# RMS norm with repeated rows: a first load in three transfers, gamma in two, one VectorE copy in two

## The chip, the cores and the metric

The kernel runs on one core of a Trainium2 chip. The core has a tensor engine (unused here), VectorE (DVE in the profile), ScalarE (ACT), GpSimd (POOL) and SyncE (SP), and 16 DMA engines that carry all traffic between HBM and the on-chip memory (SBUF, 128 partitions). DMAs are issued from an engine's own instruction queue: here SP issues the loads of x and all stores, and ACT issues the loads of gamma. The metric is the device time of one execution in microseconds (us); the number for a kernel is the median of several runs. A profile is one further execution, recorded.

## The reference

```python
def reference(x, gamma):              # x: 8 x 512 x 2048 f32, gamma: 2048 f32
    x_rep = np.repeat(x, 2, axis=1)
    rms = np.sqrt((x_rep ** 2).mean(axis=-1, keepdims=True) + 1e-6)
    x_norm = x_rep / rms
    return (x_norm * gamma[None, None, :]).astype(np.float32)
```

Each row of 2048 numbers is divided by its root mean square, multiplied by gamma, and written twice, in two neighbouring rows of the output. So 33.5 MB are read and 67.1 MB are written.

## The kernel before

**Tiling.** The 4096 rows of x are cut into four tiles of 1024. A tile puts 8 consecutive rows (`H * K`, H = 2, K = 4) on each of the 128 partitions: 64 KB of contiguous HBM per partition, 8 MB in all. A row of x becomes two output rows, so a tile makes two stores of 8 MB, one for each half `h` of its 8 rows.

**Buffers.** One SBUF array `y` holds three areas of 8 rows a partition: `first` at 0, `second` at 8, `third` at 16. The even tile of a pair is loaded at `first + K`, so its rows 0 to 3 lie in the upper half of `first` and its rows 4 to 7 in the lower half of `second`. The odd tile fills `third`. The scaled rows are written back into the same array: result row k goes to place 2k of the area that is stored, and its copy to place 2k + 1.

**Helpers.** `load` (L49 to L52) issues a tile's load on SP. Its argument `cuts` names the row numbers at which the load is cut into transfers, and the transfers are issued in reversed order, the last rows first. `squares` (L58 to L70) runs on ACT: for each row a Square with a running sum (L65, its output is thrown away in `sq`), then one Sqrt over the sums (L69). `scale` (L72 to L82) runs on VectorE: a reciprocal (L78) and, for each row, one instruction that multiplies by it and by gamma (L79). `repeat` (L84 to L86) copies finished rows to their neighbouring places, on the engine whose copy it is given, so that L86 appears for both ACT and VectorE. `store` (L54 to L57) issues a store on SP.

**Order.** The schedule is written by hand (`manual_schedule`), so instructions run on each engine in the order of the program. `four(n, constants, cuts, at_once)` handles the pair of tiles n and n + 1, and is called twice, for tiles 0 and 1 and for tiles 2 and 3. It loads the even tile, runs `constants`, loads the odd tile, and then works through four halves, each of which ends with a store: rows 0 to 3 of the even tile (in two groups of two rows), rows 4 to 7 of it in descending order, and the two halves of the odd tile. In the first two halves the copies are shared by ACT and VectorE: In the first of them ACT copies rows 0 and 1 and VectorE rows 2 and 3; in the second ACT copies rows 2 and 3 and VectorE rows 0 and 1. ACT takes `at_once` rows in an instruction, VectorE two.

**SP's queue.** SP holds, in this order, the first pair's loads, four stores, the second pair's two loads and four stores. A store waits until its copies are done. The load of tile 2 goes where the third store reads, and waits for it; the load of tile 3 likewise waits for the fourth store.

**The first call** gets `cuts` of (7, 8): row 7 of every partition goes first as a transfer of 1 MB, then rows 0 to 6 as one of 7 MB; its `at_once` is 1. The second call, for tiles 2 and 3, loads a tile in one transfer and has an `at_once` of 2 (`half`).

**Gamma** comes in through one partition and is spread to all 128 by GpSimd. `G` is 16 and `E` is 2, so `C = D // G - E` is 126. One DMA (L128) brings the first 16 x 126 = 2016 numbers, as 16 chunks of 126 in places 256 numbers apart; `E` further DMAs (L134) bring 16 numbers each. GpSimd spreads the 2016 with one broadcast (L138) and the last 32 with another (L142). The staging places lie in `y` rows 0 to 2 of partition 0, which are overwritten later by the first results. After that ACT does a Sqrt on one number (L145), for which its table is loaded.

Of the kernel before, what the change touches and what calls it, by code (L numbers as in the profile page):

```python
# [1 line left out]

# [4 lines left out]


@with_exitstack
def kernel(  # L10
    ctx: ExitStack,
    tc: tile.TileContext,
    x: bass.AP,
    gamma: bass.AP,
    out: bass.AP,
):
    nc = tc.nc
    P = nc.NUM_PARTITIONS
    f32 = mybir.dt.float32
    Act = mybir.ActivationFunctionType  # L20
    Alu = mybir.AluOpType

    B, S, D = x.shape
    Bo, So, Do = out.shape
    R = So // S
    assert R == 2 and D == Do and B == Bo and So == S * R
    eps = 1e-6
    inv_d = 1.0 / float(D)


    K = 4
    N = B * S
    ntiles = N // (P * K)
    assert N % (P * K) == 0 and ntiles == 8
    H = 2
    x_t = x.rearrange("b s d -> (b s) d").rearrange("(n p k) d -> n p k d", p=P, k=H * K)
    out_t = out.rearrange("b s d -> (b s) d").rearrange("(n p h j) d -> n h p (j d)", p=P, h=H, j=K * R)

    singles = ctx.enter_context(tc.tile_pool(name="singles", bufs=1))
    rows = ctx.enter_context(tc.tile_pool(name="rows", bufs=1))  # L40
    junk = ctx.enter_context(tc.tile_pool(name="junk", bufs=1, space=bass.MemoryType.PSUM))
    small = ctx.enter_context(tc.tile_pool(name="small", bufs=4))

    y = rows.tile([P, 3 * K * R, D], f32, name="y")
    first, second, third = 0, K * R, 2 * K * R

    def load(n, at, cuts=(H * K,)):  # L49
        ends = (0, *cuts)  # L50
        for k0, k1 in reversed(list(zip(ends, ends[1:]))):
            nc.sync.dma_start(out=y[:, at + k0 : at + k1, :], in_=x_t[n][:, k0:k1, :])  # L52

    def store(n, h, to):  # L54
        nc.sync.dma_start(
            out=out_t[n, h], in_=y[:, to : to + K * R, :].rearrange("p j d -> p (j d)")
        )  # L57

    def squares(at, rows):

        n = len(rows)
        ss = small.tile([P, n], f32, name=f"ss{n}")
        for c, k in enumerate(rows):
            sq = junk.tile([P, D], f32, name="sq")
            nc.scalar.activation(  # L65
                out=sq[:], in_=y[:, at + k, :], func=Act.Square, accum_out=ss[:, c : c + 1]
            )
        rms = small.tile([P, n], f32, name=f"rms{n}")
        nc.scalar.activation(out=rms[:], in_=ss[:], func=Act.Sqrt, scale=inv_d, bias=eps_t[:])  # L69
        return rms  # L70

    def scale(at, to, rows, rms, at_once=K):  # L72
        n = len(rows)
        rstd = small.tile([P, n], f32, name=f"rstd{n}")
        for c, k in enumerate(rows):
            if c % at_once == 0:
                part = slice(c, min(c + at_once, n))
                nc.vector.reciprocal(out=rstd[:, part], in_=rms[:, part])  # L78
            nc.vector.scalar_tensor_tensor(  # L79
                out=y[:, to + R * k, :], in0=y[:, at + k, :], scalar=rstd[:, c : c + 1],  # L80
                in1=gamma_b[:], op0=Alu.mult, op1=Alu.mult,
            )  # L82

    def repeat(to, k0, k1, copy):  # L84
        y_r = y[:, to + R * k0 : to + R * k1, :].rearrange("p (k r) d -> p k r d", r=R)
        copy(out=y_r[:, :, 1, :], in_=y_r[:, :, 0, :])  # L86

    ctx.enter_context(tc.manual_schedule())

    half = K // 2  # L90
    up, down = list(range(K)), list(range(K - 1, -1, -1))

    def four(n, constants, cuts, at_once):


        load(n, first + K, cuts)
        constants()
        load(n + 1, third)
        for rows, n_at_once in ((up[:half], half), (up[half:], at_once)):
            scale(first + K, first, rows, squares(first + K, rows), n_at_once)  # L100
        for k in range(0, half, at_once):
            repeat(first, k, k + at_once, nc.scalar.copy)
        repeat(first, half, K, nc.vector.tensor_copy)
        store(n, 0, first)
        scale(second, second, down, squares(second, down))
        for k in range(half, K, at_once):
            repeat(second, k, k + at_once, nc.scalar.copy)
        repeat(second, 0, half, nc.vector.tensor_copy)
        store(n, 1, second)
        roots = [squares(third + h * K, up) for h in range(H)]  # L110
        scale(third, first, up, roots[0])
        repeat(first, 0, half, nc.scalar.copy)
        repeat(first, half, K, nc.scalar.copy)
        store(n + 1, 0, first)
        scale(third + K, third, up, roots[1])
        repeat(third, 0, K, nc.scalar.copy)
        store(n + 1, 1, third)

    gamma_b = singles.tile([P, D], f32, name="gamma_b")
    G, E = 16, 2  # L120
    C = D // G - E
    gamma_s = y[0:1, 0:2, :].rearrange("p k (c d) -> p (k c) d", c=G // 2)
    gamma_t = y[0:1, 2, :]
    eps_t = singles.tile([P, 1], f32, name="eps_t")

    def constants():
        nc.gpsimd.memset(eps_t, eps)  # L127
        nc.scalar.dma_start(  # L128
            out=gamma_s[0:1, :, :C],
            in_=gamma[: G * C].rearrange("(p c d) -> p c d", p=1, c=G),  # L130
        )
        for c in range(E):
            at = G * C + c * G
            nc.scalar.dma_start(  # L134
                out=gamma_t[0:1, c * G : (c + 1) * G],
                in_=gamma[at : at + G].partition_broadcast(1),
            )
        nc.gpsimd.partition_broadcast(  # L138
            out_ap=gamma_b[:, : G * C].rearrange("p (c d) -> p c d", c=G),
            in_ap=gamma_s[0:1, :, :C],  # L140
        )
        nc.gpsimd.partition_broadcast(out_ap=gamma_b[:, G * C :], in_ap=gamma_t[0:1, : E * G])  # L142

        root = singles.tile([P, 1], f32, name="root")[:]
        nc.scalar.activation(out=root, in_=eps_t[:], func=Act.Sqrt)  # L145

    four(0, constants, (H * K - 1, H * K), 1)
    four(2, lambda: None, (H * K,), half)


# [1 line left out]
_INS = ['x', 'gamma']  # L152
_OUTS = [((8, 1024, 2048), 'float32')]


# [23 lines left out]
```

## Time and profile before

| what | value |
|---|---|
| median of 3 runs | 238.25 us (238.18 to 238.48) |
| profiled execution: its own time | 239.85 us |
| profiled execution: span, first to last instruction | 238.0 us |
| ACT copies of 128x4096 (6) / 128x2048 (4), mean of one | 3.598 us / 1.892 us |
| VectorE copies of 128x4096 (4), mean of one | 2.293 us |
| VectorE multiply (L79), mean of one of 32 | 2.349 us |
| load of row 7, issue to landing | 4.9 us |
| load of rows 0 to 6, issue to landing | 21.5 us |

A group of the profile is named by line, engine and operation, and what it writes and reads, with partitions x elements. An engine with a q behind its name (SPq, ACTq) is the sequencer that issues, here DMAs. A wait is shown as the idle time before an instruction and, after an arrow, what ended it. The share of the DMA engines is the mean over all 16 of them; since a window counts a packet where it begins, and a large packet takes over two microseconds, short windows go over 1.00 and under it.

### The profile page before, as it was taken

The page shows a single profiled execution, that of the slowest core. Times are in us where ns is not written, and L with a number is a line of the kernel's source. Part 1 is how long each engine was busy: PE and PEld are TensorE (multiplying, and loading weights), DVE is VectorE, ACT ScalarE, POOL GpSimd, SP SyncE. Part 2 cuts the span into 40 slices and gives each one's busy share as a digit, 9 for nine tenths or more (in the row PEclk, how much of TensorE's full clock was granted, in tenths as well). Part 3 has the DMA queues.
Part 4 walks back from the last instruction along what each step waited for, and adds up shares of the span by engine and source line. Part 5 has one row for each costly group of instructions (what it writes and reads, how often), then busy time and mean ns, then how long its engine had stood idle before and what let it go on. Part 6 is the DMA issues. An engine that isn't in the chain of part 4 may idle for free.

```text
span 238.0 us, 228 instructions
## 1 busy us (share of the span) xinstructions
DVE 84.4 (35%) x47; ACT 110.2 (46%) x88; POOL 2.9 (1%) x7
## 2 busy tenths in 40 slices
DVE  0000495792799400000000006937918992000000
ACT  2001999299996560000000039891999957400000
POOL 0300000000000000000000000000000000000000
DMA  8997989898998989898999999999998999999994
GB/s 332 463 453 340 529 352 529 352 518 363 463 419 365 518 352 529 352 529 352 419 386 430 441 441 441 430 452 408 463 419 386 474 408 463 419 441 441 441 441 176
DMA packets 1909, 100.68 MB, mean 423 GB/s; under 512 B 244, under 2 KB 244, under 8 KB 244
## 3 DMA queue, kind: packets, MB, share of 16 engines
q1 hardware_dynamic: 1872, 100.66, 98.4%
q10 hardware_dynamic: 36, 0.01, 0.0%
q14 instruction: 1, 0.01, 0.0%
HBM read 33.56 MB, written 67.11 MB: 423 GB/s over the span
## 4 chain that ended last, share of the span: by engine, by line
DMA 46%; ACT 28%; DVE 11%; issue 1%; SPq 0%; DVEq 0%; ACTq 0%
DMA y<-in_x_dram 26%; DMA out_dram<-y 20%; ACT sq L65 17%; DVE y L79 11%; ACT y L86 11%; ACT rms L69 1%; DVE rstd L78 0%; SPq L52 0%; DVEq L79 0%; ACTq L86 0%
## 5 line engine op out<-in xcount | busy, mean ns | idle before, releaser
L65 ACT ACTIVATE sq<-y 128x2048 f32<-128x2048 f32 x32 | 60.1, 1878 | 73.2 <-DMA y<-in_x_dram 72.5
L79 DVE SCALAR_TENSOR_TENSOR y<-y,rstd,gamma_b 128x2048 f32<-128x2048 f32 x32 | 73.8, 2349 | 2.2 <-DMA out_dram<-y 1.6
L86 ACT COPY y<-y 128x4096 f32<-128x4096 f32 (+2 forms) x12 | 42.8, 3599 | 18.9 <-DVE y L79 18.9
L78 DVE RECIPROCAL rstd<-rms 128x4 f32<-128x4 f32 (+2 forms) x11 | 1.9, 169 | 111.2 <-ACT rms L69 111.2
L86 DVE COPY y<-y 128x4096 f32<-128x4096 f32 x4 | 9.2, 2293 | 0.1
L65 ACT ACTIVATION_READ_ACCUMULATOR sq<-y 128x1 f32 x32 | 6.0, 186 | 0.0
L69 ACT ACTIVATE rms<-ss,eps_t 128x4 f32<-128x4 f32 (+1 forms) x10 | 3.0, 297 | 0.3
L145 ACT ACT_TABLE_LOAD x1 | 1.3, 1283 | 2.3 <-issue 2.3
L138 POOL PARTITION_BROADCAST gamma_b<-y x1 | 2.3, 2257 | 5.1 <-DMA y<-in_gamma_dram 5.1
L142 POOL PARTITION_BROADCAST gamma_b<-y x1 | 0.3, 310 | 6.2 <-DMA y<-in_gamma_dram 6.2
L145 ACT ACTIVATE root<-eps_t 128x1 f32<-128x1 f32 x1 | 0.2, 203 | 0.0
L127 POOL MEMSET eps_t<- 128x1 f32 x1 | 0.1, 98 | 0.3 <-POOLq L163 0.3
L163 POOL MEMSET const-bfloat16-1.0<- 128x1 bf16 x1 | 0.1, 101 | 0.0
L163 POOL MEMSET const-uint8-127<- 128x1 uint8 x1 | 0.1, 101 | 0.0
L163 POOL MEMSET const-float32-0.0<- 128x1 f32 x1 | 0.1, 98 | 0.2 <-issue 0.2
L163 POOL MEMSET const-float32-1.0<- 128x1 f32 x1 | 0.1, 98 | 0.0
## 6 DMA issues: line engine op xcount, KB each, us to landing
y<-in_x_dram SPq DMA_DIRECT2D x1, 7168.0 KB, 21.5
y<-in_x_dram SPq DMA_DIRECT2D x1, 1024.0 KB, 4.9
out_dram<-y SPq DMA_DIRECT2D x8, 24.9
y<-in_x_dram SPq DMA_DIRECT2D x3, 40.5
y<-in_gamma_dram ACTq DMA_DIRECT2D x2, 0.1 KB
y<-in_gamma_dram ACTq DMA_DIRECT2D x1, 7.9 KB, 5.1
```

Source lines behind the costliest of these rows:

```text
L65: nc.scalar.activation(out=sq[:], in_=y[:, at + k, :], func=Act.Square, accum_out=ss[:, c : c + 1])
L69: nc.scalar.activation(out=rms[:], in_=ss[:], func=Act.Sqrt, scale=inv_d, bias=eps_t[:])
L78: nc.vector.reciprocal(out=rstd[:, part], in_=rms[:, part])
L79: nc.vector.scalar_tensor_tensor(out=y[:, to + R * k, :], in0=y[:, at + k, :], scalar=rstd[:, c : c + 1], in1=gamma_b[:], op0=Alu.mult, op ...
L86: copy(out=y_r[:, :, 1, :], in_=y_r[:, :, 0, :])
L127: nc.gpsimd.memset(eps_t, eps)
L138: nc.gpsimd.partition_broadcast(out_ap=gamma_b[:, : G * C].rearrange("p (c d) -> p c d", c=G), in_ap=gamma_s[0:1, :, :C],)
L142: nc.gpsimd.partition_broadcast(out_ap=gamma_b[:, G * C :], in_ap=gamma_t[0:1, : E * G])
L145: nc.scalar.activation(out=root, in_=eps_t[:], func=Act.Sqrt)
L163: nc = _bacc.Bacc("TRN2", target_bir_lowering=False, num_devices=1)
```

## The change

Three things change.

1. The first call's `cuts` are (6, 7, 8): row 7, row 6 and rows 0 to 5 are loaded as three transfers in that order, of 1, 1 and 6 MB.
2. `E` is 1, so `C` is 127: the first gamma DMA brings 16 chunks of 127 numbers, one DMA brings the last 16, and GpSimd's broadcasts spread 2032 and 16 numbers.
3. VectorE's copy in the second half of the even tile is made in steps of `K - 1 - at_once` rows. That is 2 in the first call, where the copy stays one instruction, and 1 in the second call, where it becomes two instructions of one row each.

The number of DMAs in the program stays 16: one more load, one gamma transfer less.

```diff
@@ four()
         scale(second, second, down, squares(second, down))
         for k in range(half, K, at_once):
             repeat(second, k, k + at_once, nc.scalar.copy)
-        repeat(second, 0, half, nc.vector.tensor_copy)
+        step = K - 1 - at_once
+        for k in range(0, half, step):
+            repeat(second, k, k + step, nc.vector.tensor_copy)
         store(n, 1, second)
@@ gamma
-    G, E = 16, 2
+    G, E = 16, 1
     C = D // G - E
@@ calls
-    four(0, constants, (H * K - 1, H * K), 1)
+    four(0, constants, (H * K - 2, H * K - 1, H * K), 1)
     four(2, lambda: None, (H * K,), half)
```

## The prediction

> **What bounds the kernel now.** I read the page's utilisation first, then its DMA part, the timeline of instructions, and the windows view of the DMA engines last.
>
> ```profile
> DVE 84.4 (35%) x47; ACT 110.2 (46%) x88; POOL 2.9 (1%) x7
> ...
> q1 hardware_dynamic: 1872, 100.66, 98.4%
> q10 hardware_dynamic: 36, 0.01, 0.0%
> ...
> HBM read 33.56 MB, written 67.11 MB: 423 GB/s over the span
> ```
>
> No compute engine is busy half of the span, and the packets of the SP queue (q1) take 98.4% of all 16 DMA engines' time. The floor is 100.66 MB through those engines. An edit can act in two ways: it changes the work that the engines carry, or it makes a transfer reach the queue after the queue ran dry. The timeline answers the second:
>
> ```profile
> 0.72 1.34 SPq L52 DMA_DIRECT2D y<-in_x_dram  x3
> 0.72 0.60 ACTq L128 DMA_DIRECT2D y<-in_gamma_dram  x1
> 1.35 0.91 ACTq L134 DMA_DIRECT2D y<-in_gamma_dram  x2
> 2.29 1.28 ACT L145 ACT_TABLE_LOAD   x1 [2.29 <-issue]
> ...
> 14.36 0.31 POOL L142 PARTITION_BROADCAST gamma_b<-y  x1 [6.18 <-DMA y<-in_gamma_dram]
> 22.69 1.88 ACT L65 ACTIVATE sq<-y 128x2048 f32<-128x2048 f32 x1 [18.90 <-DMA y<-in_x_dram]
> ```
>
> The reader sees start, length, engine and line. All three early loads (row 7, rows 0 to 6, the whole second tile) are issued by 2.06 us; ACT's first square waits until 22.69 for rows 0 to 6. The last windows show where the DMA engines lose time (columns: stretch, length, DVE, ACT and POOL busy with counts, clock, DMA share, GB/s):
>
> ```profile
> 101.00:116.00 15.00, 0.00 (x0) 0.00 (x0) 0.00 (x0) 1.00 0.98 424
> 116.00:124.00 8.00, 0.00 (x0) 0.00 (x0) 0.00 (x0) 1.00 1.05 393
> 124.00:138.00 14.00, 0.00 (x0) 0.00 (x0) 0.00 (x0) 1.00 1.03 445
> ```
>
> At 116 to 124 the engines are full but move only 393 GB/s. There the fourth store ends and the load of tile 2 begins. The packet records say the same: a 65,536-byte packet takes 2.418 us nearly everywhere, and 2.6 to 3.9 us in this stretch. The engines, 0.4 us apart before it, leave it 1.7 us apart and end between 235.4 and 236.8 us. The last engine's last store lands at 237.17, which ends the span of 238.0.
>
> **Row 6 as a transfer of its own.** Issue: one more DMA instruction on SP, 0.37 to 0.44 us like the three there. Row 6 takes the slot at 1.14; rows 0 to 5 move to about 1.6, the second tile's load to about 2.1. Behind them SP only waits for the first store, issued at 39.29. The engines reach rows 0 to 5 when rows 7 and 6 are done, near 7.1 us (row 7's packets end at 4.6 to 5.1, and row 6 adds eight of 0.309 us): 5 us of cover, so nothing. Without cover it would be 0.42 us.
>
> Work: each engine carries 8 more packets. From the records an 8,192-byte packet takes 0.309 us and one of 57,344 bytes 2.113 us start to start. The difference, 1.804 us, is 49,152 bytes, exactly rows 0 to 5; what 8,192 bytes then take is 0.301, so 0.008 us is fixed. Rows 6 and 0 to 5 cost 0.309 + 1.812 = 2.121 against 2.113: 0.008 x 8 = 0.066 us an engine, plus one 4-byte completion packet of 0.009: **+0.075 us**. The engines never idle after it, so all of this reaches the end. Bounds: 0 from below (same bytes, same engines; a gain by shifted phases is a rival); from above +0.8 us, if row 6 starts as cold as row 7 did, whose first packets took up to 1.116 instead of 0.309. I take 0.075, since in the record rows 0 to 6 follow row 7's completion packet without a gap.
>
> A rule speaks against the split. The Trainium skill, "DMA: Bandwidth & Descriptors", section "Bandwidth", asks for at least 1 MiB a transfer and measures 6.15 us for 1 MB alone; "Anatomy of one DMA" puts about 2.0 us of fixed cost on each. Row 7 was just such a 1 MiB transfer, 4.9 us from issue to landing, but its packets were busy for 2.5 us and the next transfer's followed them at once. By the rule paid in full the sum would be about 2 us more; the trace lets the fixed part lie beside the next transfer.
>
> **Gamma.** ACT issues two DMAs instead of three: 0.21 to 0.67 us less of the stretch 0.72 to 2.26. Behind them stand the table load and a small root, then ACT is idle for 18.90 us: nothing gained. On the DMA engines, 16 packets grow from 504 to 508 bytes (0.027 us each, no change seen), and one engine loses a 64-byte packet (0.011) and its completion (0.009). Beside the small packets that engine's large ones took 2.235, 2.126, 2.125 and 2.121 us, not 2.116: 0.14 us in all. One of two such DMAs goes: half of that 0.14 and of 0.04 for its four small packets, **-0.09 us on this one engine**, bounds 0 and -0.18. It is the engine that lands last in the first load (22.67; the others by 22.39). At the end it is ahead of the next by only 0.07 us, so the end gains at most that; I take -0.02. POOL's two broadcasts are done by 14.67 and first needed at 27.35, so neither 127-wide chunks nor a shorter second broadcast reach the path; with the cover gone the second would cost its 0.31 us.
>
> **VectorE's copy.** The step K - 1 - at_once is 2 in the first call of four, which keeps one copy, and 1 in the second call: there the copy at 171.32 becomes two of 128x2048. No VectorE row has that form. Below: twice half of 2.293 us, +0. Above: two at the price of the multiply of that form, 2.349 each, +2.41. ACT's copies give 2 x 1.892 - 3.598 = +0.19, and VectorE's smallest instruction, the reciprocal, takes 0.16; I take +0.16. The sixth store's issue moves from 173.69 to 173.85. Store five's issue at 157.04 reached an engine 0.88 us later, so store six is there by 174.7; the earliest engine finishes store five at 177.3. Cover 2.6 us, enough even for +2.41. VectorE's next instruction waits anyway (5.03 us idle until 178.64). **Nothing.** With cover gone it is 0.16 us.
>
> **Sum.** The profiled execution has a span of 238.00 us and a time of its own of 239.85; the runs have a median of 238.25. +0.075 - 0.02 + 0 = +0.05 us: span 238.05, median **238.3**. The first squares move with the load, to about 22.7. Store one then arrives at 40.2 (39.29 + 0.88) where the earliest engine ends the second tile's load at 40.95; both move together, so its 0.8 us of cover stays.
>
> **Rivals.** 0.2% of 238.25 is 0.48 us, about what a measurement of this kernel can tell from no change.
>
> 1. The turn from stores to loads at 116 to 124 comes out better. The edits change by tenths of a microsecond how far the 16 engines stand apart, and that turn decides which engine ends last. For: it is the only lossy place, and the engines leave it 1.4 us apart at the end. Against: the runs shown, 238.18 to 238.48, stay within 0.30 although the start, with first packets of 0.41 to 1.12 us, looks irregular. If the loss were even, the last engine would end near the middle of 235.4 and 236.8 us, 0.7 less: 237.6, or 237.4 with what the gamma engine gains.
>
> 2. The same turn comes out worse. The quickest engines lose about 0.6 us there, the slowest 2.0 (from 99.56 to 140.22 instead of two times 19.32). If the slowest loses another 0.6 to 0.7, 238.9. It decides once the last engine loses 0.45 us more than now. For and against as above.
>
> 3. The slow side by a mechanism: a third transfer ahead of the first square starts in the open. Place: between row 7 and row 6, or row 6 and rows 0 to 5. Price: 0.8 us each if the engines start cold as at 1.7 us, 2.4 if each pays what row 7 paid beyond its packets (4.9 - 2.5), so 239.1 to 240.7. It decides once descriptors come later than 4.6 us for row 6, that is 2.6 us later than its issue plus 0.88 says. Against: no gap at the one seam that there is. The skill's fixed cost, above, would be paid here.
>
> 4. The split copy delays the sixth store: it decides from +2.6 us on 2.293, beyond the upper bound. The time would then be 238.3 plus what exceeds it. I give it no more than the rounding.
>
> That the edit does not do what it says can be only so far: the first call's copy stays whole.
>
> **How the numbers follow.** Forecast 0.64; rival 1 0.16; rival 2 0.13; rivals 3 and 4 together 0.07. Faster by over 0.2% is rival 1, 0.16; slower is rivals 2 to 4, 0.20; same 0.64. The likeliest alone gives 238.1 to 238.6 (the split 0 to 0.3, the spread of runs). The range goes down to 237.6, the middle case of rival 1, and up to 238.9, rival 2's price, leaving out rival 3 and the outer halves of the others, some 0.2.
>
> **What would show it.** Right: four loads issued on SP by about 2.5 us; 256 packets of 8,192 bytes with no gap at row 6; the first square at 22.6 to 22.8; the second gamma broadcast well before 27; two VectorE copies of 1.15 to 1.3 us near 171, the sixth store issued near 173.8; the DMA share as before. Wrong: a hole in the DMA share before 8 us, a first square after 23.4, engines dry at a store, or a last landing away from 237.2 by over 0.5 us, with the 116 to 124 stretch far from 393 GB/s.

## The result, and the profile after

The changed kernel takes 239.31 us (median of 6 runs, 239.15 to 240.19), the kernel before beside it 238.23 (6 runs, 238.03 to 238.48): a ratio of 1.0050, 95% interval 1.0034 to 1.0066. So here it is slower by 1.1 us, and the forecast of 238.3 is wrong. The profiled execution of the changed kernel has a time of its own of 239.28 us and a span of 237.5. That span is *shorter* than the 238.0 of the profile before, while the runs are longer. This contradiction is the thread that the rest follows.

First the lines that answer to those shown of before. The page of the changed kernel, utilisation, queues and traffic:

```profile
DVE 84.5 (36%) x48; ACT 110.2 (46%) x88; POOL 2.7 (1%) x7
...
q1 hardware_dynamic: 2016, 100.66, 98.5%
q10 hardware_dynamic: 34, 0.01, 0.0%
...
HBM read 33.56 MB, written 67.11 MB: 424 GB/s over the span
```

VectorE has one instruction more and the SP queue 144 packets more (128 of data, 16 completions). ACT's queue has two fewer. The timeline of its start:

```profile
0.73 0.60 ACTq L130 DMA_DIRECT2D y<-in_gamma_dram  x1
0.73 2.01 SPq L52 DMA_DIRECT2D y<-in_x_dram  x4
1.36 0.68 ACTq L136 DMA_DIRECT2D y<-in_gamma_dram  x1
2.08 1.28 ACT L147 ACT_TABLE_LOAD   x1 [2.08 <-issue]
...
7.91 0.29 POOL L144 PARTITION_BROADCAST gamma_b<-y  x1
22.58 1.88 ACT L65 ACTIVATE sq<-y 128x2048 f32<-128x2048 f32 x1 [19.01 <-DMA y<-in_x_dram]
```

Four loads are issued by 2.74 us, the second gamma broadcast runs at 7.91 instead of 14.36, and the first square starts at 22.58, not 22.69. The windows view of the start (stretch, length, DVE, ACT and POOL busy, clock, DMA share, GB/s) shows row 7 and then row 6:

```profile
2.80:4.60 1.80, 0.00 (x0) 0.76 (x2) 0.00 (x0) 1.00 1.01 423
4.60:7.00 2.40, 0.00 (x0) 0.00 (x0) 1.25 (x1) 1.00 1.00 416
```

There is no hole between them. The split copy, in the groups kept apart by form:

```profile
L86 DVE COPY y<-y 128x4096 f32<-128x4096 f32 x3 | 6.9, 2294 | 0.1
L86 DVE COPY y<-y 128x2048 f32<-128x2048 f32 x2 | 2.4, 1223 | 0.0
```

Two copies of 1.223 us stand for one of 2.294: +0.15 us, in front of a wait of VectorE. No edit costs on its own path more than was forecast, and nothing here explains 1.1 us.

### The profile page after: what moved, and what is told of

Read it like the earlier page. It is cut to its first block, busy times and chain, and to the rows that moved or that the text cites. A ratio compares the mean times of both kernels' runs of the same rounds, so it can differ in the third digit from the quotient of the medians.

```text
span 237.5 us, 228 instructions
## 1 busy us (share of the span) xinstructions
DVE 84.5 (36%) x48; ACT 110.2 (46%) x88; POOL 2.7 (1%) x7
## 4 chain that ended last, share of the span: by engine, by line
DMA 45%; ACT 27%; DVE 11%; issue 2%; SPq 0%; DVEq 0%; ACTq 0%
DMA y<-in_x_dram 26%; DMA out_dram<-y 20%; ACT sq L65 17%; DVE y L79 11%; ACT y L86 10%; ACT rms L69 1%; SPq L52 0%; DVE rstd L78 0%; DVEq L79 0%; ACTq L86 0%
## 5 line engine op out<-in xcount | busy, mean ns | idle before, releaser
L86 DVE COPY y<-y 128x4096 f32<-128x4096 f32 (+1 forms) x5 | 9.2, 1866 | 0.1
```

## Two groups of run times

**The kernel before, repeated.** The first experiment, e1, has no edit at all. (Each experiment has a label, e1 to e18; it stands where its measurement is told.)

> The kernel before once more, unchanged. Theory N (the difference of about 1.1 us lies between the kernels): 238.0 to 238.5 us and a ratio of 1.000 within 0.001. Theory V (it lies between executions, through the store-to-load turn near 116 us, and would be met by any kernel at times): single runs up to 240, ratio away from 1.000 by 0.002 or more, and a second profile in which the stretch 116 to 124 us moves another amount than 393 GB/s.

It (e1) measured 239.62 us (12 runs, 238.06 to 240.07), and the runs of the kernel before beside it 239.74 (35 runs, 238.00 to 240.18); ratio 0.9998, 0.9974 to 1.0022. Neither theory had it quite: on this chip the runs fall in two groups, with nothing between, 238.0 to 238.2 us (spans 236.2 to 236.4) and 239.4 to 240.2 (spans 237.6 to 238.3). Of the 35 runs 7 are in the lower group, of the 12 runs 2. In the first measurement, told above, the six runs of the kernel before were all in the lower one. The profile that the prediction was read from, 239.85 us and a span of 238.0, belongs to the upper one.

Each part of the change alone went beside it.

```diff
-    four(0, constants, (H * K - 1, H * K), 1)
+    four(0, constants, (H * K - 2, H * K - 1, H * K), 1)
```

> The first load in three transfers alone; gamma and the copy as before (17 DMAs). Theory L (the extra load transfer costs, by its packets and its place): 239.2 to 239.5. Theory G (gamma costs) or S (the split copy costs): 238.2 to 238.4, that is +0.075 at most, as the prediction has it.

Measured (e2): 239.48 us (11 runs, 238.82 to 239.82). No run has a span under 237.0.

```diff
-    G, E = 16, 2
+    G, E = 16, 1
```

> Gamma in two DMAs alone; load and copy as before (15 DMAs). Theory G: 239.2 to 239.5. Theories L and S: 238.1 to 238.3, the gamma engine's packets 0 to 0.18 us shorter.

Measured (e3): 240.15 us (12 runs, 238.62 to 240.53); 2 of 12 in the lower group by their spans (236.4 and 236.5).

```diff
-        repeat(second, 0, half, nc.vector.tensor_copy)
+        step = K - 1 - at_once
+        for k in range(0, half, step):
+            repeat(second, k, k + step, nc.vector.tensor_copy)
```

> VectorE's copy in two in the second call alone; 16 DMAs as before. Theory S (the split copy costs, by a wait that the profile does not show): 239.2 to 239.5. Theories L and G: 238.2 to 238.3, with the sixth store issued 0.1 to 0.2 us later behind more than 2 us of cover.

Measured (e4): 239.88 us (12 runs, 238.14 to 240.52); 4 of 12 in the lower group. By their medians none of the three tells the parts apart, since the kernel before itself was mostly in its upper group here. What differs is the share of the lower group: some with gamma or the copy alone, none of 11 with the three-part load. With a fifth to be expected, none of 11 could still be chance. The next experiments count that share, so the table, which runs ahead of them, counts runs with a span under 237 us. (e14 and e6 have shifted times and are left out, and so are the first six runs of the kernel before, whose spans are not on record; "after" is the changed kernel.)

| first load in | kernel | lower group |
|---|---|---|
| one transfer | e13 / e18 | 12 of 12 / 10 of 12 |
| one, tile 1's load in two | e17 | 8 of 12 |
| two | the kernel before, by chip, with its repeats e1 and e8 | 9 of 47, 16 of 18, 5 of 35, 6 of 29, 5 of 23 |
| two | e3, e4, e10, e12 | 2, 4, 2, 4, each of 12 |
| two, tile 2's load in two | e7 | 11 of 11, on the chip with 16 of 18 |
| three | after, e2, e5, e9, e11, e15, e16 | 1 of 71 |

The edge of 237 us is nearly clean for loads in two, not for loads in three: of the 71 runs 17 have spans of 237.0 to 237.4, where the kernel before has 2 of 134 on the four chips on which it is mostly in the upper group. So three transfers take away the runs at 236.2 to 236.6, but their own upper group begins lower.

## Where the two groups part

To see the lower group from inside, the kernel before was run once more with the profiler (e8).

> The kernel before, one look, to meet an execution of the lower group (one chance in four). Theory T: a span of 236.2 to 236.4 goes with a last engine that ends tile 2's load within 0.7 us of the first, and no packet over 3 us at 119 to 121. Theory O: such a span with the same late engines, and the time saved elsewhere. A span near 238 tells only the spread.

This execution was in the lower group: 238.28 us, span 236.5. The chain of waits has three DMA pieces late in the run; in the profile of before they read (start, length, what):

```profile
75.52 24.42 DMA out_dram<-y
...
99.95 40.61 DMA y<-in_x_dram
...
157.04 22.25 DMA out_dram<-y
```

and in e8, of the lower group:

```profile
75.21 25.11 DMA out_dram<-y
...
100.34 38.71 DMA y<-in_x_dram
...
155.52 22.23 DMA out_dram<-y
```

Tile 2's load is released at 100 us in both. It lands at 140.56 in the one and 139.05 in the other: 1.5 us, which is the difference of the spans (238.0 against 236.5). What follows has the same lengths, as the store from 157.04 and 155.52 shows. The changed kernel stands in between:

```profile
75.41 24.63 DMA out_dram<-y
...
100.05 39.99 DMA y<-in_x_dram
...
156.52 22.22 DMA out_dram<-y
```

The packet records say what happens. At 116 us the last packets of the fourth store begin, with tile 2's load right behind them (its first packets begin at 118.6 to 118.9 us). In each of the twelve profiles of the upper group one to eight packets take over 3.2 us there, in place of 2.418, and in none of the six of the lower group does one; the engines slowed most stay late to the end, and the slowest engine sets the time. Some of these profiles:

| profile | span | longest packet, store four's end | longest packet, tile 2's load begins | last engine ends |
|---|---|---|---|---|
| before | 238.0 | 3.54 | 3.87 | 236.82 |
| e1, as before | 238.1 | 3.64 | 3.31 | 236.97 |
| after | 237.5 | 3.39 | 3.31 | 236.30 |
| e5, after again | 237.5 | 3.65 | 2.95 | 236.30 |
| e10 | 237.8 | 3.61 | 2.72 | 236.57 |
| e8, as before | 236.5 | 2.90 | 2.42 | 235.22 |
| e12 | 236.2 | 2.99 | 2.57 | 234.96 |
| e13 | 236.4 | 3.04 | 2.66 | 235.19 |

In e10 a single engine, with one packet of 3.61 us, makes the upper group: all others end by 235.0. The GB/s of the 116 to 124 stretch, which the prediction leaned on, is a poor gauge of this: it counts packets where they begin, and mixes in where their starts happen to fall. The changed kernel shows

```profile
101.00:116.00 15.00, 0.00 (x0) 0.00 (x0) 0.00 (x0) 1.00 0.98 424
116.00:124.00 8.00, 0.00 (x0) 0.00 (x0) 0.00 (x0) 1.00 1.02 393
124.00:138.00 14.00, 0.00 (x0) 0.00 (x0) 0.00 (x0) 1.00 1.03 445
```

like the profile before, although its last engine is half a microsecond earlier; e14 below shows the same 393 with no slow packet at its turn, and e1, with slow packets, shows 475.

**Is it the overlap?** One more load (e6), of 64 bytes, into the third area makes SP hold tile 2's load back until the fourth store has landed:

```diff
+        if n == 2:
+            nc.sync.dma_start(out=y[0:1, third, 0:16], in_=x_t[n][0:1, 0, 0:16])
         load(n, first + K, cuts)
```

> The kernel before, with one 64-byte load into the third area ahead of tile 2's load, so that SP issues tile 2's load only when the fourth store has landed: no load runs beside a store at 116 to 124 us. Theory T (the two groups are made where reads meet the fourth store's last writes): no packet over 2.6 us near 116 to 124, the engines end within 0.6 us of each other, one group of runs only, all within 0.5; each pays a dry queue of some 1.7 to 2.3 us, so 239.8 to 240.4. Theory O (the groups come from elsewhere): still two groups 1.6 us apart, near 240 and 241.6.

Measured (e6): 241.45 us (4 runs, 241.28 to 241.87), ratio 1.0132 (1.0117 to 1.0146). The fourth store's packets take 2.42 us at most, against 2.90 in e8 and 3.65 in e5 (the changed kernel), profiled on the same chip. So in these profiles the writes are slowed only where the load stands right behind them; e14 below shows that this alone is not enough. That the four runs are one group 0.6 wide says little, since 16 of 18 runs of the kernel before were in one group on this chip too. The dry queue cost 3.2 us, not 1.7 to 2.3: the load's own first packets, started cold, took 3.0 to 3.4 us, and the engines ended 0.8 apart.

**Smaller packets at the turn.** Tile 2's load goes as row 7, then rows 0 to 6 (e7):

```diff
-    four(2, lambda: None, (H * K,), half)
+    four(2, lambda: None, (H * K - 1, H * K), half)
```

> The kernel before, with tile 2's load too cut into row 7 and rows 0 to 6, so that 8 KB packets and not 64 KB ones follow the fourth store. Theory T in the form that a late engine's first long read is what is slowed (3.0 to 3.9 instead of 2.4 us): the lateness shrinks, last engine within 0.8 us of the first, more than half of the runs under 238.5. Theory O: groups and shares as for the kernel before, 238.1 and 239.75 with a quarter low.

Measured (e7): 238.34 us (11 runs, 238.21 to 238.60), all in the lower group; ratio 0.9998 (0.9986 to 1.0011). It looks like a cure, but on that chip the kernel before was nearly always in the lower group too. The same edit on the changed kernel (e11) tests it:

> The changed kernel, with tile 2's load cut too, into row 7 and rows 0 to 6. Theory T (the 1.1 us lie at the turn from the fourth store to tile 2's load, where 64 KB reads meet the last writes): all runs at 238.2 to 238.7, with no late engine, though the first load keeps its three transfers. Theory F (they are lost at the first load or in the first half): still 239.2 to 239.5.

Measured (e11): 239.43 us (12 runs, 239.07 to 239.93), none in the lower group. Theory T in that form falls. Its profile still has a packet of 3.42 us at the end of the fourth store: there it is the store's last writes that are slowed, with 8 KB reads behind them as with 64 KB ones.

## What the change does to the share

The changed kernel went again beside the kernel before, on the chip of e6, e7 and e8, where the latter was nearly always in the lower group:

> The changed kernel again, beside many more runs of the kernel before. Runs so far show two groups for the kernel before, 238.0 to 238.2 and 239.5 to 240.2 us, and one, 239.2 to 240.2, for the changed one. Theory M (the row 6 transfer keeps the kernel out of the lower group): no run, or one in twelve, under 238.5, while the kernel before has some 25% there; medians within 0.4 of each other. Theory C (both kernels draw from the same two groups, and the first comparison met a low streak): about a quarter of the runs at 238.0 to 238.4.

Measured (e5): 239.35 us (6 runs, 238.43 to 239.55), one in six in the lower group; the kernel before 238.27 (17 runs), 15 in it. Ratio 1.0040 (1.0026 to 1.0054). That repeats the first result. It speaks for theory M against C, though not by all its signs: the kernel before had 15 of 17 low and not a quarter, and the medians lie 1.1 apart. On a chip where both are mostly in the upper group the three transfers cost nothing:

> The first load in three transfers alone, once more. Theory L (the transfer of row 6 keeps the kernel in the upper group): at least 10 of 12 runs over 238.8 us, whatever share of the kernel before is low on this chip. Theory C (chance, or the chip): the same share of low runs as the kernel before beside it.

Measured (e9): 239.51 us (12 runs, 239.08 to 240.13), none in the lower group; the kernel before 239.73 (35 runs), 5 in it. Ratio 1.0005 (0.9983 to 1.0027). Within the upper group the three-part load is even the quicker by some 0.2 us, and that makes up for the low runs that it lacks: the means are 239.55 and 239.53, as they were 239.44 and 239.43 in e2 and beside it. So the 1.1 us of the first result are met only where the kernel before is mostly in the lower group.

The changed kernel with its first load in two again (e10):

```diff
-    four(0, constants, (H * K - 2, H * K - 1, H * K), 1)
+    four(0, constants, (H * K - 1, H * K), 1)
```

> The changed kernel with its first load in two transfers again, row 7 and rows 0 to 6; gamma in two and the split copy stay. Theory L: the groups and shares of the kernel before, 0 to 0.4 us higher. Theories G or S (gamma's transfers or the copy keep it in the upper group): at least 10 of 12 runs over 238.8.

Measured (e10): 239.81 us (12 runs, 238.39 to 240.23), 2 of 12 in the lower group, like the kernel before beside it (5 of 35). Two transfers, but cut between rows 5 and 6 (e12):

```diff
-    four(0, constants, (H * K - 1, H * K), 1)
+    four(0, constants, (H * K - 2, H * K), 1)
```

> The kernel before, its first load cut into rows 6 and 7 as one transfer of 2 MB, then rows 0 to 5: the bytes stand as in the changed kernel, the number of transfers as in the kernel before. Theory K (the number of transfers on the SP queue ahead of tile 2's load, seven or eight, decides the group): shares as for the kernel before. Theory B (how many bytes go in the first transfers decides): as for the changed kernel, at least 10 of 12 over 238.8.

Measured (e12): 239.44 us (12 runs, 237.99 to 240.04), 4 of 12 in the lower group, as theory K has it. So it is not where the bytes are cut that matters, but into how many transfers. That left the question what the number acts through.

**One transfer (e13).**

```diff
-    four(0, constants, (H * K - 1, H * K), 1)
+    four(0, constants, (H * K,), 1)
```

> The kernel before with its first load in one transfer: six transfers on the SP queue ahead of tile 2's load. Theory K7 (only seven ahead lets the lower group occur): no run, or one in twelve, under 238.6. Theory K8 (eight or more shut it out) and theory R (three transfers shut it out): low runs at least as often as the kernel before beside it. The start may add or save some 0.3 us.

Measured (e13): 238.53 us (12 runs, 238.44 to 238.85), the kernel before 239.59 (29 runs); ratio 0.9961 (0.9943 to 0.9980). All 12 in the lower group, so theory K7 falls. The chain shows tile 2's load landing at 138.95:

```profile
0.72 22.00 DMA y<-in_x_dram
...
75.56 24.52 DMA out_dram<-y
...
100.15 38.80 DMA y<-in_x_dram
```

**Eight transfers on the SP queue, the first load in two (e14).**

```diff
         constants()
+        if n == 0:
+            nc.sync.dma_start(out=y[:, third, 0:16], in_=x_t[n + 1][:, 0, 0:16])
         load(n + 1, third)
```

> The kernel before with one more small SP load (128 partitions of 64 bytes, into the third area ahead of tile 1's load, overwritten by it): eight transfers and eight packets an engine more ahead of tile 2's load, the first load in two as before. Theories K7 and K8: no run, or one in twelve, under 238.6. Theory R (the three transfers of the first load themselves): shares as for the kernel before. Tile 1's load waits for the small one to land, at about 22 us, so about 2 us of dry queue may come on top of both groups; the two are then told by their distance of 1.6.

Measured (e14): 242.04 us (6 runs, 241.58 to 242.22), one group. Tile 1's load waited as foreseen, but ended near 45.4 us instead of 41.2, which costs about 4 us and not 2: besides the dry queue, 15 of its 16 first packets were slow (2.9 to 3.4 us), and the last packet of each of the 16 engines, at 41.4 to 42.0 us with the first store behind it, took 3.3 to 4.1 us. The turn from stores to loads, now near 120 us, has no slow packet (2.48 at most), though the load stands right behind the store. So eight transfers do not bring the slow writes by themselves; since the dry queue moved everything, and slowed another turn, this speaks against K8 but does not settle it. Three transfers of other sizes (e15):

```diff
-    four(0, constants, (H * K - 1, H * K), 1)
+    four(0, constants, (K, K + 2, H * K), 1)
```

> The kernel before with the first load in three transfers of other sizes: rows 6 and 7, rows 4 and 5, rows 0 to 3. Theories K7, K8 and R: no run, or one in twelve, under 238.6. Theory B (8 KB packets in the second place, as row 6 alone makes them): shares as for the kernel before.

Measured (e15): 239.39 us (12 runs, 239.06 to 240.33), none in the lower group: theory B falls. Three transfers, row 7's on ACT's queue (e16):

```diff
+            issue = nc.scalar if len(cuts) == 3 and k1 == H * K else nc.sync
-            nc.sync.dma_start(out=y[:, at + k0 : at + k1, :], in_=x_t[n][:, k0:k1, :])
+            issue.dma_start(out=y[:, at + k0 : at + k1, :], in_=x_t[n][:, k0:k1, :])
```

> The three transfers of the changed kernel, with row 7's issued by ACT and not SP; gamma and copy as before. Seven transfers on the SP queue ahead of tile 2's load. Theories K7 and K8: shares as for the kernel before. Theory R: no run, or one in twelve, under 238.6.

Measured (e16): 239.60 us (12 runs, 239.17 to 240.18), none in the lower group with seven on SP's queue, where the kernel before, with seven too, has 6 of 29. So the count on that queue is hardly it; theory R, the number of transfers in the first load, has held wherever the groups could be told apart. The cut moved to tile 1's load, with the first in one (e17):

```diff
-        load(n + 1, third)
+        load(n + 1, third, (H * K - 1, H * K) if n == 0 else (H * K,))
```

> The first load in one transfer, and tile 1's load cut into row 7 and rows 0 to 6: seven transfers ahead of tile 2's load, as in the kernel before, but the cut 20 us later. Theory A (the cut acts at the start): nearly all runs in the lower group, within 0.5 us of each other at 238.2 to 238.9. Theory N (any cut ahead of the turn acts): two groups 1.6 us apart, at least half of the runs in the upper one.

Measured (e17): 238.41 us (12 runs, 238.08 to 240.02), 8 in the lower group and 4 in the upper; the kernel before 239.65 (23 runs, 5 in the lower). Between the two theories: a cut later acts too, but less. Last, the changed kernel with its first load in one transfer (e18):

> The changed kernel with its first load in one transfer; gamma in two and the split copy stay. Theory L (of the change, the first load's transfers alone cost): nearly all runs in the lower group, 238.1 to 238.9 by what lies outside the span, so at or below the kernel before's fastest and some 1 us below the changed kernel. Theories G or S: 239.2 to 240.

Measured (e18): 238.62 us (12 runs, 238.51 to 239.36), ratio 0.9968 (0.9951 to 0.9986). Ten of 12 are in the lower group, two just above it at spans of 237.0 and 237.2. So of the change it is the first load's transfers that cost; gamma's and the copy do not keep the kernel out of the lower group. e13 and e18 are also quicker than both kernels where the kernel before is mostly in its upper group, though not quicker than its lower group.

**Still open** is the way from the cut to the turn: why the number of transfers at 1 to 2 us bears on whether a packet is slowed 115 us later, when all engines have long run at one pace, and why one chip of those met had the kernel before in the lower group in 16 of 18 runs (as it was in 6 of 6 of the first measurement) and the other four in 14 to 22%. How far the engines stand apart does not tell it: the last packets of the fourth store start within 0.54 us in the profile before and 0.49 in e1, of the upper group, and within 0.52, 0.80 and 0.81 in e12, e8 and e13, of the lower. One rival to theory R is also left: the number of transfers of x and of the output ahead of tile 2's load on both queues together. With six, 22 of 24 runs are low, with seven about a fifth on four chips (8 of 12 in e17), with eight 1 of 71. e17 shows that the place of the cut counts as well, and e14, the one test of the number alone, was disturbed.

## Why the prediction was wrong

- **What bounds the kernel**: right. The DMA engines do, and in the profile shown the only place after the start that loses much is the turn at 116 to 124 us.
- **Row 6, +0.075 us**: the seam has no gap, as forecast, and the fourth load was issued by 2.74 us (2.5 forecast). Rows 0 to 5 end at 21.82 us on the mean engine, against 21.83 for rows 0 to 6 before and 21.85 and 21.91 in e2 and e9: 0.0 to 0.1 us, within what starts differ by. Rival 3, a fixed cost in the open, did not occur: the windows show row 6 at 416 GB/s behind row 7 at 423. Of the two rules that the prediction cites against the split, one does not speak against it: the Trainium skill ("DMA: Bandwidth & Descriptors", "Bandwidth") asks for transfers of at least 1 MiB, and row 6, with 128 pieces of 8 KB, is just that. The other is the fixed cost of about 2.0 us, which the Trainium skill gives ("DMA: Bandwidth & Descriptors", "Anatomy of one DMA") for DMAs that GpSimd issues. SP issues these, and no such cost lies in the open between rows 7 and 6.
- **Gamma**: of no use at the end, as forecast. The size of -0.09 us is not shown: the first load's last engine lands at 22.56 us instead of 22.67, but the kernel before lands at 22.54 in e1 and 22.37 in e8.
- **VectorE's copy**: +0.16 forecast, 2 x 1.223 - 2.294 = +0.15 measured, hidden as forecast.
- **The sum** was made against the profiled execution, 239.85 us, and laid on a median of 238.25. That these lie 1.6 us apart was stated and not asked about. It was the sign that the profile shows the slowed turn and the runs shown do not.
- **The step that failed** is the turn from stores to loads at 116 to 124 us, which the sum put at nothing, as if its loss were the same in every execution and in both kernels, and which rival 2 priced at 238.9 with a chance of 0.13. "The runs shown, 238.18 to 238.48, stay within 0.30" was held against a different outcome of the turn, but these are all from the lower group, and the profile whose turn was read is from the upper. So the price set a further loss on a turn already slowed. Counted from an undisturbed turn it is 1.1 to 1.6 us, so 239.3 to 239.9; with three transfers in the first load 70 runs of 71 lie above the lower group, most of them near that price. That rival 2 named the place was right. Its reason, that the edits change how far the engines stand apart, is not borne out: at the turn they stand 0.5 to 0.9 us apart in profiles of the upper group and 0.5 to 0.8 in those of the lower. What links the edit to the turn stays open.
- **Rival 4** did not occur. Rival 1 could not: the turn of the runs shown had no loss to save.

## What to carry to other kernels

Set the profiled execution's own time beside the runs before reading anything from it: where they differ by more than the runs' spread, the profile shows another case than the number to be predicted. When 16 engines run full to the end, the time is that of the slowest one, so look at the longest packets where the traffic turns from stores to loads, not at the mean share. An edit that costs nothing on the path can still change how often such a straggler occurs; then count the runs in each group, on more than one chip, before believing a median: here the same edit costs 1.1 us on one chip and nothing by the median on others.

## What the runs showed of the hardware beyond that

- **A turn from writes to reads can slow single engines**: packets of 64 KB that take 2.418 us nearly everywhere else took up to 3.65 us as the last writes of a store with the next load right behind them, and 2.42 at most when the load was held back (e6). In e14 they took 2.42 to 2.48 with the load right behind.
- **A turn from reads to writes can, too**: the last reads of tile 1's load, at about 39 us with the first store behind them, took up to 3.0 us in all four profiles of the chip of e5 to e8 (14 to 17 packets over 2.5 us, 5 at most in the other profiles but e14), and 3.3 to 4.1 us in e14. As e5 is of the upper group and e8 of the lower, this does not decide the group.
- **The time outside the span is not constant**: a run's time less its span is 1.8 us for the kernel before, the changed one, e2, e5, e9, e10 and e17, but 1.9 to 2.0 for e4, e6, e14 and e15, and 2.1 to 2.2 for e3, e13 and e18. It is steady for each program within 0.1. No count of transfers or instructions orders it (e3 and e10 have 15 transfers each and lie 0.35 apart); what sets it was not tried. It is why e13, with spans like the lower group of the kernel before (236.3 against 236.2), takes 238.53 and not 238.1.
- **Eight 64 KB packets an engine start cold at 2.9 to 3.3 us for the first** (e13, near 1.7 us), against 0.41 to 1.12 for 8 KB ones; the whole first load lands hardly later for it, at 22.72 us against 22.67 in the profile before and 22.37 in e8.
